# Recurrent chain of a bidirectional RWKV-7 mixer: matrix products regrouped by the form of the array they use, heads alternating, one PSUM bank for each direction's y

## The chip, the cores and the metric

One core of one Trainium2 chip runs the whole kernel. The metric is the device time of one execution in microseconds, as the median of several runs.

## The reference, cut to what matters

The reference runs two layers of a backbone over 256 context and 256 latent tokens (width 1024). Each layer has a SwiGLU half step, three mixers side by side (mLSTM, RWKV-7, differential attention) with a gated merge, and a second SwiGLU half step. The change touches only the RWKV-7 mixer. For each of 8 heads of width 64 and for each of two directions it runs this recurrence over the tokens, first over the context, then over the latent tokens:

```python
def step(s, inp):
    rt, wt, kt, vt, kkt, at = inp
    sa = jnp.einsum('bhvk,bhk->bhv', s, -kkt)
    s = s * wt[:, :, None, :] + sa[..., None] * (kkt * at)[:, :, None, :] + vt[..., None] * kt[:, :, None, :]
    return s, jnp.einsum('bhvk,bhk->bhv', s, rt)
```

The outputs of the two directions are added. The backward direction goes through the context from its end to its start and then through the latent tokens the same way.

## The kernel before, in words

The 512 tokens are cut into 8 chunks of 64 (chunks 0 to 3 context, 4 to 7 latent). The 8 heads are worked on as 4 tiles of two heads: head 0 on partitions 0 to 63, head 1 on 64 to 127. For each tile t four parts follow one another: `rwkv_cols` (dense projections), `rwkv_stage1` (elementwise work and a few products), `rwkv_stage2` (the score products "A", masks and transposes), `rwkv_solve` (a triangular inverse, mostly on VectorE), and `rwkv_chain`, the recurrence over chunks. `rwkv_post` ends the tile.

`rwkv_stage2` makes for each direction d, each half g of the chunks and each head h one PSUM bank pA: four products with a contraction over the 64 partitions of the head and 128 columns (shown by the profile as 64\*128). Three VectorE instructions then mask it into Z, Ma and Mr. The bank comes from the tag "c", which has two buffers.

`rwkv_chain` takes 8 steps; step i works on chunk i of the forward direction and on the matching chunk of the backward one. A step is: X = Ma·UV + ar·S (products of 64 by 64, one for each head and direction, shown as 64\*64), a VectorE copy of X, U = Bt·X (64\*64), two copies of U into UV (VectorE for head 0's half, ScalarE for head 1's), the state products S from UV and BK (contraction over 128 partitions, 64 columns, shown as 128\*64), and two VectorE instructions that make the next S. The output y of a chunk is Mr·UV (128\*64) plus ar·S (64\*64), accumulated in PSUM; then VectorE adds it to `ry` or ScalarE copies it there. y is written as a function `out` that is kept in `pending` and called in the next step behind the products of X. In the second layer y is wanted for latent tokens only: steps 0 to 3 have none. Each fp32 product is two matmul instructions with a weight load each.

PSUM has eight banks by tag: two "d", three "m", two "c", one "s". In the chain X, U, S and Y all take "c". The "s" bank serves `rwkv_stage1` (its products kkn, lw, la).

The order of the instructions on each engine is not written by hand: a scheduler goes through the program with a priority for each instruction and a model of time, and emits for each engine a fixed order. The chain, `rwkv_stage1` and `rwkv_solve` stand under `tc.high_priority()`; the other work of the layer (attention, mLSTM, gate tiles, merge; all dense products go through L102) is emitted in portions, `run(BUDGET[l][t][0])` and `[1]`, and fills TensorE where the chain isn't ready. What is left runs in `run(1e9)` behind the last chain. `mm` at L102 issues all products but those of U (L1116) and of the solve (L1067, L1080).

Of the kernel before, what the change touches and what calls it, by code (L numbers as in the profile page):

```python
# [35 lines left out]
# columns of the packed per-partition parameters  # L36
# [3 lines left out]
# columns of the packed constants  # L40
# [10 lines left out]
# per layer: gate tiles after each attention and mLSTM head; other work (in us of TensorE) before and after  # L51
# the columns of each next recurrent tile
# [28 lines left out]
class Halves:  # L81
    """a unit's 1024 columns in two tiles"""
# [9 lines left out]
class Builder:  # L92
# [36 lines left out]
    def unit(self, spec):  # L129
        """hi and lo parts of a unit; exact together"""  # L130
# [16 lines left out]
    def unit_early(self, spec):  # L147
        """a unit in room that the feed-forward part doesn't need yet"""
        raw = self.fp.tile([P, 1024], F32, name="araw", tag="araw", bufs=4)
        self.unit_load(raw, spec)  # L150
        r = []
        for i, tag in enumerate(("uh", "ul")):
            r.append(Halves([self.fp.tile([P, 1, NT], F32R, name=tag, tag=tag, bufs=14) for _ in range(2)]))
        for n in range(2):
            c = slice(n * NT, (n + 1) * NT)
            self.split(r[0][:, c], r[1][:, c], raw[:, c])
        return r
# [4 lines left out]
    def fm_tile(self, spec, lo=0, h=None, ps=None):  # L162
        """one feature-major tile of 128 columns: PSUM [128 cols, tokens]"""
# [17 lines left out]
    def fm_first(self, units, pss, parts):  # L181
        """the first tiles after a norm: every feature block goes to all of them as soon as it is there"""
# [10 lines left out]
    def split(self, hi, lo, src):  # L193
        """exact split of src: hi carries the leading half of the significand"""
        self.nc.scalar.copy(hi, src)
        self.nc.vector.tensor_tensor(lo, src, hi.bitcast(F32), op=ALU.subtract)  # L196

    def rsqrt(self, out, in_, eps, scale=1.0):
        """out = 1/sqrt(scale*in + eps)"""
# [8 lines left out]
    def ada_first(self, i, j):  # L208
        """block j of modulation vector i (0 shift, 1 scale) of the first norm, on TensorE"""
# [18 lines left out]
    def ada_first_shift(self, j):  # L228
        """the shift on VectorE"""
# [13 lines left out]
    def load_c(self, after=lambda: None):  # L243
        """silu of the two condition vectors on every partition"""
# [23 lines left out]
    def ada_steps(self):  # L268
        """the others on VectorE: one block of 128 outputs at a time"""
# [27 lines left out]
    def sqrt_ahead(self):  # L297
        """has ScalarE's table for the square roots of the next norm loaded before they are due"""
# [4 lines left out]
    def sumsq(self, k, c):  # L303
        """adds the squares of x_k to the running sum of these tokens"""
# [9 lines left out]
    def norm_stats(self, parts):  # L314
        """1 / rms of these tokens on every partition, in PSUM"""
# [16 lines left out]
    def norm_apply(self, l, i, k, psr, parts):  # L332
        """feature block k of the modulated norm, split into hi and lo"""
# [12 lines left out]
    def norm_mod(self, l, i, parts):  # L346
        """norm and modulation of these tokens"""
# [5 lines left out]
    def x_update(self, l, gi, k, ps, c):  # L353
        """x_k += 0.5 * gate * ps"""
# [12 lines left out]
    def ffn(self, l, which, lo, ready, after):  # L367
        """ready: the PSUM tiles of the first gate and up tiles;
        after: token ranges with what to do when x has its final value there"""
# [60 lines left out]
    def conv(self, out, ps, w, lo=0):  # L430
        """out = centred 3-tap convolution of ps; w: three [128,1] taps"""
# [35 lines left out]
    def tm_group(self, cols, consume, t0=0):  # L467
        """token-major product with 256 columns (cols: (c0, width) ranges): PSUM [128 tokens, 256]
        for each of the token tiles from t0 on"""
# [19 lines left out]
    def attn_qk(self, h):  # L489
        """raw q and k of a head, token-major (token tile, q or k), and the sums of their squares"""  # L490
# [14 lines left out]
    def attn_qk_pair(self, hp):  # L505
        """the same for two heads without the context's q: slots k0 k1 q2 k2 q3 k3 of the token tiles"""
# [32 lines left out]
    def attn_rot(self, qkr, ss):  # L539
        """normalised and rotated q and k of a head, feature-major"""  # L540
# [104 lines left out]
    def mlstm_steps(self):  # L645
# [21 lines left out]
        # gates: rows 0-3 i fwd, 32-35 i bwd, 64-67 f fwd, 96-99 f bwd (others zero)  # L667
# [27 lines left out]
        # m = F + G; em = exp(-m); nG = -G, its hi part on the first half of the partitions, lo on the other  # L695
# [20 lines left out]
        for h in range(4):  # L716
# [16 lines left out]
            # s-block j: scores against the query tokens it can reach  # L733
# [9 lines left out]
            for j in range(4):  # L743
# [3 lines left out]
                for d in range(2):  # L747
                    # reachable query blocks
# [66 lines left out]
    def rwkv_small(self):  # L815
# [6 lines left out]
        # hi and lo parts of a direction on the two halves of the partitions  # L822
# [59 lines left out]
    def rwkv_stage1(self, t, r, k, v, lw, g2):  # L882
        """everything that is elementwise over (channel, token)"""
# [5 lines left out]
        # normalised keys  # L889
# [5 lines left out]
        # 1 / max(norm, 1e-12)  # L895
# [50 lines left out]
    def rwkv_stage2(self, t, r, k, v, g2, kk, eC, dirs):  # L946
# [6 lines left out]
        # token-major v and the u of each chunk: head 0 has v on partitions 0-63 and u on 64-127,  # L953
        # head 1 the other way round. Token window w is tokens 64w-64 .. 64w+64
# [6 lines left out]
        for d in range(2):  # L961
# [6 lines left out]
            for g in range(2):  # L968
                for h in range(2):
                    pA = self.psc("A")  # L970
                    hr = slice(64 * h, 64 * h + 64)
                    for n in range(4):
                        c = 4 * g + n
                        self.mm(pA[:, n * P : (n + 1) * P], bk[hr, c].rearrange("p a b -> p (a b)"),
                                ar[hr, d, c].rearrange("p a b -> p (a b)"), True, True)
                    pv4 = pA.rearrange("p (n x) -> p n x", n=4)
# [24 lines left out]
        # bonus  # L1001
# [7 lines left out]
    def rwkv_solve(self, t, Zf):  # L1009
        """Bt[(h, s), (d, c), t] = transpose of (I - A)^-1, A strictly triangular in (t, s)"""  # L1010
        nc, a = self.nc, self.a2
        Bt = self.Bts[t % 2]
        # Zf[(h, s), (d, c), t]: the diagonal blocks first
# [7 lines left out]
        # backward units: transpose within the block so that every unit is strictly lower in (row, col)  # L1021
# [6 lines left out]
        # two sets of columns in turn, so that VectorE always has an independent instruction  # L1028
# [13 lines left out]
        # back: R[row, u, col]  # L1042
# [6 lines left out]
        # forward units: Rn = T (t, s), Rt = T^T; backward units: Rn = T^T, Rt = T  # L1049
# [5 lines left out]
        # off-diagonal blocks  # L1055
# [33 lines left out]
    def rwkv_chain(self, t, g2, Mr, Ma, BK, UV, ar, eC, bon):  # L1089
# [7 lines left out]
        S = pending = None  # L1097
        for i in range(8):
            cs = [order[0][i], order[1][i]]
            px = self.psc("X")  # L1100
            for d in range(2):
                c = cs[d]
                for h in range(2):
                    hr = slice(64 * h, 64 * h + 64)
                    self.mm(px[hr, d * 64 : d * 64 + 64], Ma[hr, d, c], UV[hr, c, h], True, i == 0)
                    if i:
                        self.mm(px[hr, d * 64 : d * 64 + 64], ar[hr, d, c, 0], S[hr, d], False, True)
            if pending:
                pending()
            X = a.tile([P, 2, 64], F32, name="X", tag="X", bufs=2)  # L1110
# [8 lines left out]
            both = (lambda x: x[:, cs[0] :: st][:, 0:2]) if st > 0 else (lambda x: x[:, cs[0] :: st][:, 0:2])  # L1119
# [9 lines left out]
            def out(i=i, cs=cs, S=S):  # L1129
                if cs[0] < lc and cs[1] < lc:  # L1130
                    return
                py = self.psc("Y")
                for d in range(2):
                    c = cs[d]
                    for h in range(2):
                        hr = slice(64 * h, 64 * h + 64)
                        self.mm(py[hr, d * 64 : d * 64 + 64], UV[:, c, h], Mr[:, d, c, h], True, i == 0)
                        if i:
# [429 lines left out]
```

## Time and profile before

| | |
|---|---|
| median of 3 runs | 2867.44 us (2856.05 to 2876.06) |
| span of the profiled execution | 2880.2 us |
| TensorE busy | 2784.9 us, 97% |
| VectorE busy | 1862.6 us, 65% |
| ScalarE busy | 1146.1 us, 40% |

The profiled execution has no time of its own beside its span; the span is 12.8 us above the median of the runs and 4.1 us above the slowest of them. A matmul counts as busy from its start until its result is in PSUM, so a busy TensorE isn't one at its peak. The two mixer stages lie at about 426 to 1238 us (layer 0) and 2026 to 2700 us (layer 1).

### The profile page before, as it was taken

To read this page: it belongs to the slowest core of one execution; us is meant where nothing else is said; L and a number is where in the kernel's file an instruction comes from. 1 tells how busy PE (TensorE), PEld (TensorE's weight loads), DVE (VectorE), ACT (ScalarE), POOL (GpSimd) and SP (SyncE) were. 2 spreads that over 40 slices of the span, in tenths; PEclk is the share of its full clock that TensorE was granted. 3 is DMA by queue.
4 is the path that set the end of the run, shared out by engine and by line. 5 is a ranking of instruction groups with operands and counts; after the bars stand their busy time and mean duration, and the time that the engine had idled before them with its cause. 6 is when DMAs were issued, how large, how long until landed. Compare 5 with 4: busy or idle time off the path is not lost.

```text
span 2880.2 us, 43519 instructions
## 1 busy us (share of the span) xinstructions
PE 2784.9 (97%) x17198; PEld 2280.8 (79%) x17198; DVE 1862.6 (65%) x3611; ACT 1146.1 (40%) x1955; POOL 236.5 (8%) x330
## 2 busy tenths in 40 slices
PE   7999999999999999999999999999999899998999
PEld 5888887668676677688888888888878677878999
DVE  7999368474593663589995443333877677746654
ACT  3322244443553543343222332222554546444543
POOL 0000002111110200200000000000212121112000
PEclk9999999799997999999999999999989899989999
DMA  7777322111121222666773232222221121226454
GB/s 264 237 238 227 100 94 68 34 63 39 59 75 41 70 74 80 225 205 221 237 240 109 88 102 96 95 95 74 98 78 57 61 65 57 92 92 214 162 183 147
DMA packets 102432, 349.65 MB, mean 121 GB/s; under 512 B 13362, under 2 KB 17842, under 8 KB 101972
## 3 DMA queue, kind: packets, MB, share of 16 engines
q1 hardware_dynamic: 91872, 315.10, 33.5%
q0 software_dynamic: 9024, 31.60, 3.3%
q8 instruction: 135, 2.21, 0.3%
q14 instruction: 69, 0.57, 0.1%
q10 hardware_dynamic: 1332, 0.18, 0.0%
HBM read 327.82 MB, written 19.01 MB: 120 GB/s over the span
## 4 chain that ended last, share of the span: by engine, by line
PE 60%; DVE 8%; issue 4%; ACT 3%; DMA 2%; POOL 1%; DVEq 0%; POOLq 0%; ACTq 0%; SPq 0%
PE d L102 25%; PE m L102 22%; PE Y L102 2%; PE A L102 2%; DVE lo L144 1%; PE X L102 1%; DVE op L1038 1%; DVE T L1041 1%; DMA yin<-yd 1%; DMA raw<-in_ws 1%; PE mo L102 1%; PE aS L102 1%; PE S L102 1%; PE U L1116 1%; ACT hi L140 1%
## 5 line engine op out<-in xcount | busy, mean ns | idle before, releaser
L140 ACT CAST hi<-raw 128x1024 fp32r<-128x1024 f32 x430 | 451.0, 1049 | 1022.0 <-PE m L102 468.0
L144 DVE TENSOR_TENSOR lo<-raw,hi 128x1024 fp32r<-128x1024 f32 (+1 forms) x508 | 544.6, 1076 | 322.7 <-ACT hi L140 315.6
L102 PE MATMUL m<-hh,hi 128*128 128x512 f32 (+1 forms) x1440 | 510.8, 357 | 3.9 <-ACT hh L342 2.5
L102 PE MATMUL m<-hl,hi 128*128 128x512 f32 (+1 forms) x1440 | 513.2, 357 | 0.0
L102 PE MATMUL m<-hh,lo 128*128 128x512 f32 (+1 forms) x1440 | 512.5, 357 | 0.0
L102 PE MATMUL d<-hh,hi 128*128 128x256 f32 (+1 forms) x976 | 357.5, 367 | 4.0 <-DVE x L359 2.7
L102 PE MATMUL d<-hl,hi 128*128 128x256 f32 (+1 forms) x976 | 353.1, 362 | 0.4 <-DVE hl L196 0.4
L102 PE MATMUL d<-hh,lo 128*128 128x256 f32 (+1 forms) x976 | 349.1, 358 | 0.1
L239 DVE SCALAR_TENSOR_TENSOR ajunk<-araw,scb 128x1024 f32<-128x1024 f32 x272 | 332.5, 1222 | 5.1 <-ACT scb L266 0.5
L102 PEld LDWEIGHTS m<-hh,hi 128*128 128x128 f32 x1440 | 272.0, 190 | 45.3 <-ACT hh L342 3.1
L102 PEld LDWEIGHTS m<-hh,lo 128*128 128x128 f32 x1440 | 272.8, 190 | 40.2 <-DVE lo L144 0.2
L102 PEld LDWEIGHTS m<-hl,hi 128*128 128x128 f32 x1440 | 272.8, 190 | 39.9 <-issue 0.2
L102 PE MATMUL d<-ul,hi 128*128 128x512 f32 (+1 forms) x770 | 269.3, 350 | 0.0
L102 PE MATMUL d<-uh,hi 128*128 128x512 f32 (+1 forms) x770 | 268.5, 349 | 0.0
L102 PE MATMUL d<-uh,lo 128*128 128x512 f32 (+1 forms) x770 | 268.3, 349 | 0.0
L102 PEld LDWEIGHTS d<-hh,hi 128*128 128x128 f32 x976 | 191.9, 197 | 37.5 <-issue 8.2
L102 PEld LDWEIGHTS d<-hl,hi 128*128 128x128 f32 x976 | 191.7, 196 | 34.5 <-issue 12.7
L102 PEld LDWEIGHTS d<-hh,lo 128*128 128x128 f32 x976 | 191.9, 197 | 26.3 <-issue 5.1
L102 PEld LDWEIGHTS d<-uh,hi 128*128 128x128 f32 x770 | 145.1, 188 | 20.8
L102 PEld LDWEIGHTS d<-ul,hi 128*128 128x128 f32 x770 | 145.4, 189 | 19.7
L102 PEld LDWEIGHTS d<-uh,lo 128*128 128x128 f32 x770 | 144.9, 188 | 19.9
L102 PE MATMUL d<-lo,hh 128*128 128x256 f32 x480 | 142.9, 298 | 0.0
(357 smaller groups left out, 4268.3 us busy)
## 6 DMA issues: line engine op xcount, KB each, us to landing
raw<-in_ws SPq DMA_DIRECT2D x430, 512.0 KB, 3.4
araw<-in_ws SPq DMA_DIRECT2D x146, 512.0 KB, 4.4
gd<-gth POOLq DMA_DIRECT2D x24, 256.0 KB, 2.5
gth<-gd SPq DMA_DIRECT2D x24, 256.0 KB, 2.9
xd<-x POOLq DMA_DIRECT2D x2, 2048.0 KB, 7.9
gd<-gth POOLq DMA_DIRECT2D x24, 128.0 KB, 2.0
gth<-gd SPq DMA_DIRECT2D x24, 128.0 KB, 3.3
yin<-yd POOLq DMA_DIRECT2D x11, 256.0 KB, 4.6
```

What stands on the lines that cost most here:

```text
L102: self.nc.tensor.matmul(out, lhsT=lhsT, rhs=rhs, start=start, stop=stop)
L140: self.nc.scalar.copy(hi, raw)
L144: self.nc.vector.tensor_tensor(lo[:, c], raw[:, c], hi[:, c].bitcast(F32), op=ALU.subtract)
L239: self.nc.vector.scalar_tensor_tensor(junk, raw, 1.0, self.scb[:, st], op0=ALU.mult, op1=ALU.mult, accum_out=self.mods[l][:, s, k, st : st ...
L1038: nc.vector.tensor_tensor(w, A[:, i + 1 :, i : i + 1].broadcast_to(w.shape), T[:, i : i + 1, c].broadcast_to(w.shape), op=ALU.mult)
L1041: nc.vector.tensor_tensor(t, t, w, op=ALU.add)
L1116: self.nc.tensor.matmul(pu[ur, d * 64 : d * 64 + 64], lhsT=Bt[hr, 8 * d + cs[d]], rhs=X[hr, d], start=True, stop=True, tile_position=(hr.s ...
```

## The change

Three places change; comments and docstrings are dropped too, so line numbers move.

- `rwkv_stage2`: for each direction and half, the banks of both heads are taken at once, and the heads alternate from product to product. The three VectorE instructions of each bank follow as before.
- X: for each direction first ar·S of both heads, then Ma·UV of both heads (before: for each head Ma·UV, then ar·S).
- y: Mr·UV of both directions is issued right behind the state products of the same step. ar·S follows in the next step behind the products of X, with the copies (function `y_state`). Each direction's y has its own bank: one from "c", one from "s".

```diff
@@ rwkv_stage2
             for g in range(2):
+                pAs = [self.psc("A") for _ in range(2)]
+                for n in range(4):
+                    c = 4 * g + n
+                    for h in range(2):
+                        hr = slice(64 * h, 64 * h + 64)
+                        self.mm(pAs[h][:, n * P : (n + 1) * P], bk[hr, c].rearrange("p a b -> p (a b)"),
+                                ar[hr, d, c].rearrange("p a b -> p (a b)"), True, True)
                 for h in range(2):
-                    pA = self.psc("A")
                     hr = slice(64 * h, 64 * h + 64)
-                    for n in range(4):
-                        c = 4 * g + n
-                        self.mm(pA[:, n * P : (n + 1) * P], bk[hr, c].rearrange("p a b -> p (a b)"),
-                                ar[hr, d, c].rearrange("p a b -> p (a b)"), True, True)
-                    pv4 = pA.rearrange("p (n x) -> p n x", n=4)
+                    pv4 = pAs[h].rearrange("p (n x) -> p n x", n=4)
@@ rwkv_chain
+        def y_state(py, cs, S):
+            if S is not None:
+                for d in range(2):
+                    for h in range(2):
+                        hr = slice(64 * h, 64 * h + 64)
+                        self.mm(py[d][hr, :64], S[hr, d], ar[hr, d, cs[d], 1], False, True)
+            for d in range(2):
+                c = cs[d]
+                if c in seen:
+                    nc.vector.tensor_tensor(y[:, c], y[:, c], py[d][:, :64], op=ALU.add)
+                else:
+                    nc.scalar.copy(y[:, c], py[d][:, :64])
+                    seen.add(c)
...
             px = self.psc("X")
             for d in range(2):
                 c = cs[d]
+                if i:
+                    for h in range(2):
+                        hr = slice(64 * h, 64 * h + 64)
+                        self.mm(px[hr, d * 64 : d * 64 + 64], ar[hr, d, c, 0], S[hr, d], True, False)
                 for h in range(2):
                     hr = slice(64 * h, 64 * h + 64)
-                    self.mm(px[hr, d * 64 : d * 64 + 64], Ma[hr, d, c], UV[hr, c, h], True, i == 0)
-                    if i:
-                        self.mm(px[hr, d * 64 : d * 64 + 64], ar[hr, d, c, 0], S[hr, d], False, True)
+                    self.mm(px[hr, d * 64 : d * 64 + 64], Ma[hr, d, c], UV[hr, c, h], i == 0, True)
             if pending:
                 pending()
+                pending = None
...
-            def out(i=i, cs=cs, S=S):
-                if cs[0] < lc and cs[1] < lc:
-                    return
-                py = self.psc("Y")
+            if not (cs[0] < lc and cs[1] < lc):
+                py = [self.psc("Y"), self.pss("Y")]
                 for d in range(2):
-                    c = cs[d]
                     for h in range(2):
                         hr = slice(64 * h, 64 * h + 64)
-                        self.mm(py[hr, d * 64 : d * 64 + 64], UV[:, c, h], Mr[:, d, c, h], True, i == 0)
-                        if i:
-                            self.mm(py[hr, d * 64 : d * 64 + 64], S[hr, d], ar[hr, d, c, 1], False, True)
-                for d in range(2):
-                    c = cs[d]
-                    if c in seen:
-                        nc.vector.tensor_tensor(y[:, c], y[:, c], py[:, d * 64 : d * 64 + 64], op=ALU.add)
-                    else:
-                        nc.scalar.copy(y[:, c], py[:, d * 64 : d * 64 + 64])
-                        seen.add(c)
-            pending = out
+                        self.mm(py[d][hr, :64], UV[:, cs[d], h], Mr[:, d, cs[d], h], True, i == 0)
+                if i:
+                    pending = lambda py=py, cs=cs, S=S: y_state(py, cs, S)
+                else:
+                    y_state(py, cs, None)
```

## Rows read from the trace of the kernel before

**Rows 1.** The page's first part: busy time, share of the span, instructions.

```profile
PE 2784.9 (97%) x17198; PEld 2280.8 (79%) x17198; DVE 1862.6 (65%) x3611; ACT 1146.1 (40%) x1955; POOL 236.5 (8%) x330
```

**Rows 2.** Windows: length, busy PE, PEld, DVE, ACT, POOL, granted clock, DMA, GB/s.

```profile
426.00:1238.00 812.00, 777.53 (x4987) 582.33 (x4986) 492.32 (x1078) 354.52 (x685) 118.79 (x146) 0.93 0.24 78
1113.00:1238.00 125.00, 118.78 (x511) 91.98 (x510) 68.34 (x110) 47.35 (x80) 25.21 (x33) 0.99 0.59 190
676.00:730.00 54.00, 54.00 (x477) 39.63 (x477) 21.41 (x59) 13.43 (x36) 4.53 (x4) 1.00 0.13 45
790.00:890.00 100.00, 91.53 (x561) 68.10 (x559) 75.43 (x160) 51.82 (x90) 11.33 (x17) 0.91 0.20 67
1070.00:1113.00 43.00, 43.00 (x400) 29.01 (x399) 12.90 (x38) 7.56 (x21) 2.54 (x5) 1.00 0.18 59
2026.00:2700.00 674.00, 636.86 (x4963) 531.48 (x4963) 471.91 (x1119) 337.23 (x637) 111.73 (x163) 0.92 0.29 93
```

**Rows 3.** Timeline of one chain step, layer 1: start, us, engine, line, out<-in.

```profile
2580.46 0.26 ACT L1122 COPY UV<-U 64x128 f32<-64x128 f32 x1 [0.81 <-DVE UV L1121]
...
2581.37 0.45 PE L102 MATMUL S<-UV,BK 128*64 128x64 f32 x6
2581.75 0.33 PE L102 MATMUL X<-UV,Ma 64*64 64x64 f32 x2
...
2582.00 0.39 PE L102 MATMUL d<-hh,lo 128*128 128x256 f32 x1
2582.18 0.29 DVE L1158 TENSOR_TENSOR S<-S,eC 128x128 f32<-128x128 f32 x1
...
2582.55 0.33 PE L102 MATMUL Y<-Mr,UV 128*64 128x64 f32 x2
2582.81 0.33 PE L102 MATMUL Y<-ar,S 64*64 64x64 f32 x2
2583.07 0.33 PE L102 MATMUL Y<-Mr,UV 128*64 128x64 f32 x2
...
2583.33 0.27 PE L102 MATMUL X<-S,ar 64*64 64x64 f32 x1
...
2584.15 0.29 DVE L1111 COPY X<-X 128x128 f32<-128x128 f32 x1 [1.68 <-PE X L102]
...
2585.30 0.28 PE L102 MATMUL d<-hh,hi 128*128 128x256 f32 x1
2585.51 0.45 PE L1116 MATMUL U<-X,Bt 64*64 64x64 f32 x8
2585.89 0.39 PE L102 MATMUL d<-hl,hi 128*128 128x256 f32 x1
...
2586.11 0.28 PE L102 MATMUL d<-hh,lo 128*128 128x256 f32 x1
2586.23 0.28 PE L102 MATMUL m<-yh,hi 128*128 128x256 f32 x1
```

**Rows 4.** Windows of tile Y alone, both mixer stages: PE, PEld, DVE, ACT.

```profile
426.00:1238.00 812.00, 64.45 (x480) 44.89 (x480) 5.63 (x32) 5.32 (x32) 0.93 0.24 78
2026.00:2700.00 674.00, 34.39 (x256) 24.25 (x256) 2.82 (x16) 2.62 (x16) 0.92 0.29 93
```

**Rows 5.** Windows of tile A alone, sum of both mixer stages (PE first).

```profile
sum 1486.00, PE 72.80 PEld 62.12 DVE 161.79; mean PE 36.40 PEld 31.06 DVE 80.89
```

**Rows 6.** Instructions on tile A: count, ns min/median/max, first and last start.

```profile
L979 DVE TENSOR_TENSOR Z<-A,cst x64: 417/423/427, 449.9 to 2497.0; 64x256 f32<-64x256 f32 x64
...
L983 DVE TENSOR_TENSOR Mr<-A,cst x64: 403/416/426, 450.7 to 2497.9; 128x256 f32<-128x256 f32 x64
```

**Rows 7.** Timeline of TensorE at 1021 us, two blocks of A.

```profile
1021.60 1.71 PE L102 MATMUL A<-ar,bk 64*128 64x128 f32 x16
1023.24 0.38 PE L102 MATMUL d<-hi,hh 128*128 128x256 f32 x1
...
1024.12 1.13 PE L102 MATMUL A<-ar,bk 64*128 64x128 f32 x8
```

More of the change, by code (lines that the diff above doesn't have):

```diff
@@ L1118, in rwkv_chain @@
             st = cs[1] - cs[0]
-            both = (lambda x: x[:, cs[0] :: st][:, 0:2]) if st > 0 else (lambda x: x[:, cs[0] :: st][:, 0:2])
+            both = lambda x: x[:, cs[0] :: st][:, 0:2]
             pu2 = pu[:, :128].rearrange("p (d x) -> p d x", d=2)
@@ L1159, in rwkv_chain @@
                 S = Sn
-        pending()
+        if pending:
+            pending()
         return t, y, g2, bon
```

## Prediction

> **What bounds the kernel now.** I read the page's busy times first: TensorE 97% of the span, VectorE 65%, ScalarE 40% [rows 1]. Busy says little by itself, so the next view is the table of windows [rows 2]. In windows that hold only the chain, TensorE has no idle time at all (54.00 of 54 us, 43.00 of 43), while VectorE works in 40% and 30% of them. In a window of score products and solve (790 to 890 us) TensorE idles 8.5 us of 100 and VectorE works 75. Over both mixer stages the idle time is 34 and 37 us of 812 and 674. Behind layer 0's last chain there are still 125 us of dense work, 119 of them busy. So the mixer stages are bound by TensorE's queue, nearly everywhere.
>
> The timeline of one step shows what that queue spends its time on, and that the recurrence waits for it rather than the reverse [rows 3]. UV is complete at 2580.72 (2580.46 + 0.26), and the last six state products start at 2581.37: 0.65 us in the queue. The state is updated at 2582.47, the first product of X with it starts at 2583.33: 0.86 us. The copy of X ends at 2584.44, U starts at 2585.51: 1.07 us. That is 2.58 us a step by which TensorE is late. What I take out of the queue shortens the step until these three are used up.
>
> In the same rows y is the costly part. Its products go two by two, Mr·UV (128\*64), ar·S (64\*64), Mr·UV, and each pair of instructions starts 0.26 us after the pair before. The eight instructions of U, which have one form and alternate heads, take 0.45 us together, of which one lasts 0.27 by itself (as the first X product): 0.18 / 7 = 0.026 us for each further one. A change of form costs TensorE far more than the products do.
>
> **The change, part by part.** First the price of a block that stands alone between dense products [rows 3]. Dense products start 0.12 us apart (2586.11 to 2586.23). Into U it is 0.21 (0.09 more), U to the next dense one 0.38, and the dense one after that 0.22 (0.10 more): 0.57 us. Eight instructions that join a block of their own form cost 8 x 0.026 = 0.21.
>
> *y.* Steps with both parts: 7 for each of 4 tiles in layer 0, 4 for each of 4 in layer 1 = 44; the counts agree, 480 and 256 instructions (the first step of layer 0 has eight) [rows 4]. Before, a step costs 4 x 0.52 (2582.55 to 2583.07) + 0.09 + 0.10 = 2.27 us. 44 of them are 100 us, and the windows show 64.45 + 34.39 = 98.84. After, Mr·UV is ready at the moment the state products are (both need UV alone) and has their form: 0.21. ar·S uses the old state, so nothing holds it until the next X; a scheduler that takes what is ready puts it right behind Mr·UV, a block alone: 0.57. Together 0.78, which saves 1.49 x 44 = 66 us. Ends: both alone, 1.14, 50 us; both joined (ar·S with X), 0.42, 81 us. I take 66.
>
> *X.* Today two instructions of Ma·UV go ahead, while the state is being updated: 0.25 us from 2581.75 to 2582.00. With ar·S first they can't, and join X's block: 2 x 0.026. That is 0.20 x 56 steps (7 in each of 8 chains) = 11 us. Ends 0 and 11. I take 11. Nothing is late for it: X needed the state before, too.
>
> *A.* The 64 blocks of eight are busy for 72.80 us, 1.14 each [rows 5]. Where the last products of one head met the first of the next, sixteen took 1.71 instead of 1.13 + 8 x 0.123 (0.123 being (1.13 - 0.27) / 7) = 2.11 [rows 7]: two heads run at the same time on the two halves of the rows. With full alternation sixteen should take what eight take now, 32 blocks instead of 64, 37 us less. But VectorE needs three instructions for each bank, two kinds of which take 0.42 us [rows 6]; 3 x 0.42 = 1.26 is more than TensorE's 1.13, and with both banks of "c" taken at once TensorE can't fill one while the other is drained. So the stage isn't shorter, and only dense work that happens to be ready turns the freed time to use; in the window of such a stage 8.5% was idle already. Ends 0 and 37; I take half, 18, since dense work was ready for most but VectorE has little room.
>
> A rule of the Trainium skill speaks against this part. TensorEngine Tiling (Array Packing), section PSUM Bottleneck, says that packing speeds up the products and not the emptying of PSUM, which may then bound. The rows agree so far (1.26 against 1.13); by the rule A would give 0, and the sum would be 18 less.
>
> *Banks.* U now takes the bank of "c" that y's first direction leaves, so U waits for its copy. Behind U on TensorE everything waits. If y's copy is late each time by one such copy (0.26, as the UV copy), that is 44 x 0.26 = 11 us; if ar·S runs early, 0. I take 5. The second direction holds "s" from behind S until at most the next U (2581.37 to 2585.51, 4.1 us), which `rwkv_stage1` uses for five products. That collides where stage 1 of the next tile runs beside a chain with y. At worst 5 x 4.1 = 21 us in a tile, but as a delay of the recurrence, and the 125 us of dense work behind layer 0's last chain cover it: 0. Without that cover the 21 us would count. The copies of y are as many as before. No DMA, SyncE or GpSimd instruction moves.
>
> *Sum.* 66 + 11 + 18 - 5 = 90 us, 3.1% of the profiled span. 2880.2 - 90 = 2790; the median of the runs lies 12.8 below that span, so 2867.4 - 90 = **2777 us**. Per step with y about 1.7 us leave the queue, less than the 2.58 by which it is late, so the recurrence doesn't become the bound.
>
> **The rivals.** *VectorE keeps A's gain.* The mechanism is above: 1.26 us of masks for a bank against 1.13 of products. For it: VectorE works 75 of 100 us there. Against: the idle time of TensorE is only 8.5. It gives 66 + 11 - 5 = 72, so 2795.
>
> *The blocks don't stay together.* The scheduler orders by its own model; it already splits the state products (six of the eight stand in one row, two went ahead). If it splits Mr·UV and ar·S likewise with dense work between, a piece of two costs 0.25 + 0.09 + 0.10 = 0.44, one of six 0.57 - 0.05 = 0.52, so y costs 1.92 a step and saves 0.35 x 44 = 15; the X gain is lost the same way. 15 + 18 - 5 = 28, so 2839. Against: the state products split because the second head's UV comes later, and Mr·UV has both.
>
> *The clock, slower than before.* The granted clock is 0.93 and 0.92 over the mixer stages: (1 - 0.93) x 2 x 812 + (1 - 0.92) x 2 x 674 = 222 us at 1.2 GHz instead of 2.4 [rows 2]. The chain windows in the rows have 1.00, the solve's window 0.91. If chains with tighter small products count as quiet like the solve, some 340 us more of the chains (8 of about 50 us, part of them low already) go to 1.2 GHz; each such microsecond loses half: +170 - 90 = +80, 2947. It decides from 180 us more at 1.2 GHz, that is a granted clock of 0.865 in place of 0.925. Against: the change removes stalls between products and adds none.
>
> **How the numbers follow.** Forecast 0.58 (own range 2755 to 2805: y between its ends, A between 10 and 30), A's gain kept by VectorE 0.20, blocks apart 0.14, clock 0.08. A measurement of this kernel tells about 1% from no change: faster is below 2839. The first two and half of the third are faster: 0.85; the other half the same: 0.07; slower 0.08. With the upper ends of y, X and A (81 + 11 + 37) the time would be 2738; the range is 2750 to 2838, which leaves out the clock, half of the blocks apart and the joined ends.
>
> **What would show it.** After the change: Mr·UV right behind the state products in one run of 128\*64; y's busy sum at about 98.84 x 0.78 / 2.27 = 34 us; blocks of sixteen A in about 1.15 us; no early pair of Ma·UV; chain steps with y shorter by about 1.7 us; TensorE still without idle time in chains. I would be wrong if the blocks are scattered, if U waits visibly for a copy of y, if TensorE's idle time in score stages grows by what A frees, or if the granted clock falls.

## The result and the profile after

The change takes 2797.45 us in the median of 4 runs (2791.73 to 2807.59) against 2871.22 for the kernel before, measured beside it (4 runs, 2856.05 to 2876.06): a ratio of 0.9742, 95% interval 0.9700 to 0.9784. The forecast was 2777, range 2750 to 2838. So direction and range held; 90 us were forecast and 74 came. What the 74 are made of is another matter than the prediction said. Its rival "VectorE keeps A's gain" had named almost this time, 2795, but TensorE spent hardly less on A, so there was no gain for VectorE to keep (see the experiments on A).

The first part of the page after answers to [rows 1]:

```profile
PE 2689.3 (96%) x17198; PEld 2220.3 (79%) x17198; DVE 1855.8 (66%) x3611; ACT 1145.2 (41%) x1954; POOL 237.5 (8%) x330
```

TensorE is busy 95.6 us less (2784.9 to 2689.3), but the span is only 74.4 shorter (2880.2 to 2805.8): its idle time grew by 21.2, from 95.3 to 116.5. The windows of the two mixer stages, which answer to the first and last of [rows 2], show where:

```profile
425.00:1190.00 765.00, 723.20 (x5001) 547.54 (x5000) 494.69 (x1081) 356.54 (x688) 118.59 (x146) 0.95 0.25 83
1976.00:2660.00 684.00, 632.25 (x5244) 541.78 (x5244) 485.07 (x1141) 352.50 (x659) 112.97 (x163) 0.94 0.31 101
```

Idle 41.8 and 51.8 us, where it was 34 and 37; and the granted clock is 0.95 and 0.94 in place of 0.93 and 0.92. Tile Y in the same windows (compare [rows 4]) is busy for 29.72 + 17.19 = 46.91 us; it was 98.84, and 34 was forecast:

```profile
425.00:1190.00 765.00, 29.72 (x480) 23.99 (x480) 5.94 (x32) 5.60 (x32) 0.95 0.25 83
1976.00:2660.00 684.00, 17.19 (x256) 13.56 (x256) 3.07 (x16) 2.62 (x16) 0.94 0.31 101
```

One chain step of layer 1 on TensorE (timeline, compare [rows 3]):

```profile
2541.07 0.45 PE L1138 MATMUL U<-X,Bt 64*64 64x64 f32 x8
...
2542.24 0.33 PE L102 MATMUL S<-UV,BK 128*64 128x64 f32 x2
2542.41 0.28 PE L102 MATMUL Y<-Mr,UV 128*64 128x64 f32 x2
2542.62 0.39 PE L102 MATMUL d<-hh,lo 128*128 128x256 f32 x1
2542.93 0.39 PE L102 MATMUL S<-UV,BK 128*64 128x64 f32 x5
2543.10 0.22 PE L102 MATMUL Y<-Mr,UV 128*64 128x64 f32 x1
2543.15 0.22 PE L102 MATMUL S<-UV,BK 128*64 128x64 f32 x1
2543.16 0.45 PE L102 MATMUL Y<-Mr,UV 128*64 128x64 f32 x5
2543.54 0.45 PE L102 MATMUL Y<-ar,S 64*64 64x64 f32 x8
2543.92 0.39 PE L102 MATMUL d<-hh,hi 128*128 128x256 f32 x1
...
2545.07 0.33 PE L102 MATMUL X<-S,ar 64*64 64x64 f32 x4
...
2545.46 0.28 PE L102 MATMUL X<-UV,Ma 64*64 64x64 f32 x4
2545.68 0.39 PE L102 MATMUL d<-hh,lo 128*128 128x256 f32 x1
...
2546.34 0.45 PE L1138 MATMUL U<-X,Bt 64*64 64x64 f32 x8
```

As forecast: Mr·UV joins S, from 2542.93 to 2543.54 twelve instructions of one form in a row (four went ahead; by the program they are head 0's, whose half of UV is copied first); ar·S follows at once as a block of eight, long before X; X is sixteen instructions in 0.61 us (2545.07 to 2545.68) with no early pair of Ma·UV; nothing waits for a copy of y.

**Two measures for what follows.** Runs of one and the same kernel differ, and by their clock: in 22 runs of the kernel before, the time goes from 2857.34 us at a granted clock of 0.971 to 2885.81 at 0.961. A run's time multiplied by its clock is an estimate of what it would take at 2.4 GHz throughout, if all that runs at 1.2 GHz took half as long there. I call it the time at full clock. For one kernel it hardly moves: over those 22 runs it is 2774.0 with a standard deviation of 2.7, and in two later sets of 11 and 10 runs 2774.0 and 2774.9. So each time splits into work and clock: before 2774.0 and 98 lost to the clock (2871.8 - 2774.0, mean of the 22); after 2725.1 and 73.5 (mean 2798.6). The gain of 73 between these means is 49 of work and 24 of clock.

The second measure splits TensorE's time by tile: from each instruction's start to the next one's, without the idle part, each stretch multiplied by the clock granted in it, summed over the profiled execution (us; one execution of each kernel):

| | Y | S | X | A | idle |
|---|---|---|---|---|---|
| before | 85.5 | 30.5 | 51.3 | 64.9 | 87.8 |
| after | 39.3 | 22.3 | 36.7 | 63.2 | 107.1 |
| y alone | 41.7 | 22.4 | 47.3 | 64.5 | 108.8 |
| X alone | 86.5 | 32.2 | 37.2 | 65.4 | 94.1 |
| A alone | 84.2 | 31.4 | 52.4 | 63.3 | 92.4 |
| y and X | 39.3 | 22.3 | 36.5 | 65.0 | 101.3 |
| A forced to alternate | 40.1 | 21.4 | 36.2 | 46.6 | 117.0 |
| one bank for y | 37.4 | 25.8 | 37.5 | 64.9 | 90.1 |
| heads in turn | 41.9 | 22.7 | 52.9 | 62.6 | 104.6 |

### The profile page after: what moved, and what is told of

Its sections match the earlier page's. It is cut to its first block, busy times and chain, and to the rows that moved or that the text cites. A ratio compares the mean times of both kernels' runs of the same rounds, so it can differ in the third digit from the quotient of the medians.

```text
span 2805.8 us, 43561 instructions
## 1 busy us (share of the span) xinstructions
PE 2689.3 (96%) x17198; PEld 2220.3 (79%) x17198; DVE 1855.8 (66%) x3611; ACT 1145.2 (41%) x1954; POOL 237.5 (8%) x330
## 4 chain that ended last, share of the span: by engine, by line
PE 79%; DVE 10%; ACT 4%; issue 3%; DMA 2%; POOL 2%; ACTq 0%; DVEq 0%; POOLq 0%; SPq 0%
PE d L102 33%; PE m L102 32%; PE A L102 2%; PE X L102 1%; DVE lo L144 1%; PE Y L102 1%; PE mo L102 1%; DVE op L1041 1%; DVE T L1044 1%; PE S L102 1%; PE aS L102 1%; PE U L1138 1%; DMA yin<-yd 1%; DVE bk L942 1%; PE ay L102 1%
## 5 line engine op out<-in xcount | busy, mean ns | idle before, releaser
L102 PE MATMUL d<-hh,hi 128*128 128x256 f32 (+1 forms) x976 | 349.7, 358 | 3.7 <-ACT tw L824 0.8
L102 PE MATMUL d<-hl,hi 128*128 128x256 f32 (+1 forms) x976 | 344.0, 353 | 0.2 <-DVE hl L196 0.2
L102 PEld LDWEIGHTS d<-hh,hi 128*128 128x128 f32 x976 | 186.9, 191 | 36.5 <-issue 9.8
L102 PEld LDWEIGHTS d<-hl,hi 128*128 128x128 f32 x976 | 186.9, 191 | 31.4 <-issue 11.0
L102 PEld LDWEIGHTS d<-hh,lo 128*128 128x128 f32 x976 | 186.8, 191 | 31.4 <-issue 7.2
L102 PE MATMUL d<-hi,hh 128*128 128x256 f32 x480 | 147.3, 307 | 3.2 <-DVE mz L439 3.2
```

Of the source, the lines that this page charges most:

```text
L102: self.nc.tensor.matmul(out, lhsT=lhsT, rhs=rhs, start=start, stop=stop)
```

## The experiments

All of them are measured beside the kernel before. The kernels' times (clock and time at full clock are means over the runs):

| | median us (runs) | ratio to before, 95% | clock | at full clock |
|---|---|---|---|---|
| y alone | 2838.88 (6) | 0.9903 (0.9877 to 0.9929) | 0.966 | 2743.5 |
| X alone | 2855.73 (11) | 0.9934 (0.9903 to 0.9965) | 0.971 | 2766.5 |
| A alone | 2857.90 (12) | 0.9952 (0.9930 to 0.9974) | 0.973 | 2779.9 |
| y and X | 2817.30 (5) | 0.9826 (0.9795 to 0.9856) | 0.966 | 2719.8 |
| A forced to alternate | 2824.91 (5) | 0.9807 (0.9777 to 0.9837) | 0.960 | 2712.2 |
| one bank for y | 2773.02 (6) | 0.9621 (0.9589 to 0.9654) | 0.978 | 2711.7 |
| y and X, heads of A swapped | 2805.34 (6) | 0.9750 (0.9715 to 0.9784) | 0.970 | 2723.5 |
| all, heads of A swapped | 2798.33 (6) | 0.9713 (0.9683 to 0.9742) | 0.971 | 2717.7 |
| one bank, without A | 2801.65 (6) | 0.9751 (0.9701 to 0.9800) | 0.969 | 2716.8 |
| one bank, A forced | 2797.80 (6) | 0.9738 (0.9696 to 0.9781) | 0.968 | 2707.2 |
| heads in turn | 2809.98 (4) | 0.9782 (0.9718 to 0.9846) | 0.977 | 2743.9 |
| one bank, ar·S behind X | 2774.62 (6) | 0.9665 (0.9619 to 0.9711) | 0.977 | 2712.3 |

### The parts by themselves

**y alone.** X and A as in the kernel before.

```diff
-                if i:
-                    for h in range(2):
-                        self.mm(px[hr, ...], ar[hr, d, c, 0], S[hr, d], True, False)
                 for h in range(2):
-                    self.mm(px[hr, ...], Ma[hr, d, c], UV[hr, c, h], i == 0, True)
+                    self.mm(px[hr, ...], Ma[hr, d, c], UV[hr, c, h], True, i == 0)
+                    if i:
+                        self.mm(px[hr, ...], ar[hr, d, c, 0], S[hr, d], False, True)
...
-                pAs = [self.psc("A") for _ in range(2)]
+                    pA = self.psc("A")
```

> Only the y part of the change: Mr·UV behind S, ar·S as a block, a bank for each direction; X and A as before. Theory (runs of one form): in the order that TensorE is given, the short products of the chain stand in 626 runs of one form before (351 of 64*64, 275 of 128*64), 283 after, and here in 328 (223 and 105), so 298 of the 343 runs that the change removes are gone. The tiles X, S, U and Y took 212 us from start to start before and 134 after, 78 for 343 runs, 0.23 each. So 298 x 0.23 = 68 us less TensorE time in the chains here, and with the part that turned into idle time after, a time of about 2871 - 50 = 2815 to 2825. By the prediction's own term (66) 2805. Rival (the clock carries it): the granted clock rose from 0.93/0.92 to 0.95/0.94 in the mixers after; if that came from X or A, it is 0.93/0.92 here and the gain is under 40, above 2830.

It missed: 2838.88, not 2815 to 2825. Y and S fell by 43.8 and 8.1 and X by 4.0, 56 of the 68 us expected of TensorE; 21 us came back as idle time, and 30.5 at full clock are left. The clock stayed at 0.966. The rival's time came true, and its reason in part: some of the whole change's gain is clock, and it isn't y that brings it. The other part of the miss is the idle time, which the rival did not name.

**X alone.** The kernel before with the order of X from the change.

```diff
                 for h in range(2):
-                    self.mm(px[hr, ...], Ma[hr, d, c], UV[hr, c, h], True, i == 0)
-                    if i:
-                        self.mm(px[hr, ...], ar[hr, d, c, 0], S[hr, d], False, True)
+                    self.mm(px[hr, ...], Ma[hr, d, c], UV[hr, c, h], i == 0, True)
```

> Only the X part: ar·S of both heads, then Ma·UV of both heads; y and A as before. Theory: the short products stand in 578 runs of one form instead of 626, 48 x 0.23 = 11 us, and the X products alternate heads in pairs: 2855 to 2863. The prediction's term gives the same 11, 2860. Rival: without the early Ma·UV the step gets longer where X was already waited for; then no gain, 2871.

2855.73, as expected. X itself fell by 14.1, at full clock the kernel by 7.5, since 6 us came back as idle time. The rest of the time's gain is clock, which in these 11 runs goes from 0.964 to 0.981, further than in the runs of any other kernel.

**A alone.** The kernel before with `rwkv_stage2` from the change:

```diff
+                pAs = [self.psc("A") for _ in range(2)]
+                for n in range(4):
+                    for h in range(2):
+                        self.mm(pAs[h][:, ...], bk[hr, c]..., ar[hr, d, c]..., True, True)
```

> Only the score products A regrouped; chain as before. Theory: the scheduler undoes the alternation, because the two banks of c come free one after the other: in the order given to TensorE, A stands in 53 blocks before and 53 here, of one head each. Then the time is that of before, 2871 within 6 us, and A stays busy for 72 to 77 us in all. The prediction's term would give 18 less, 2853. Rival (taking both banks at once holds the stage up): slower by up to 10.

Neither theory: 2857.90, a gain of 0.5% with an interval clear of 1. But A hardly got cheaper (64.9 to 63.3), and at full clock the kernel is 5.9 slower. What it gained is clock: 0.970 to 0.975 in its 12 runs, 0.961 to 0.971 in the 22 of before.

**y and X.** The change without that diff.

> The change without its A part. Theory: A's part is worth nothing (its blocks stand in the same order), so this kernel takes the time of the whole change, 2797 within 6 us. By the prediction's term of 18 for A: 2815. If holding both banks costs something: under 2792.

2817.30, so the term of 18 seemed to hold after all. At full clock, though, this kernel is at 2719.8, no worse than the whole change (2725.1); all that it lacks is clock, 0.966 against 0.974.

### A: work or clock?

**A forced to alternate.** Edges hold the sixteen products of two banks in the order head 0, head 1, head 0, ...

```diff
                     for h in range(2):
-                        self.mm(pAs[h][:, ...], bk[hr, c]..., ar[hr, d, c]..., True, True)
+                        ins = self.mm(pAs[h][:, ...], bk[hr, c]..., ar[hr, d, c]..., True, True).ins
+                        if last is not None:
+                            self.tc.add_manual_dep(ins, last.name, NoSync, reason="alternate")
+                        last = ins
```

> The whole change, with edges that force the order of the score products: head 0, head 1, head 0, ... in each pair of banks, so that the heads really alternate. In these numbers time at full clock is a run's time multiplied by its granted clock (before 2774, the change 2725). Theory (A is a cost of TensorE): sixteen instructions take what eight took, A falls from 63 us at full clock to about 35 and the time at full clock to about 2700, 2775 us at a clock of 0.974. Rival (VectorE keeps the gain, 1.26 us of masks for a bank against 1.13 of products; both banks must be free first): A falls as well, but idle time grows by as much, and the time at full clock stays at 2725 or rises to 2740.

Without the edges nearly all of A stands as before, in blocks of eight or two such blocks in a row (54 blocks with A alone, 53 before). The reason that I give for it is an argument from the program and not from a run: the two banks of c come free one after the other, and the scheduler issues what is ready, all products of the first bank, then all of the second. With the edges the timeline shows fourteen instructions in the time that eight took [rows 7]:

```profile
446.50 0.46 PE L102 MATMUL A<-ar,bk 64*128 64x128 f32 x2 [0.21 <-DVE bk L942]
...
448.19 1.13 PE L102 MATMUL A<-ar,bk 64*128 64x128 f32 x14 [0.68 <-DVE bk L942]
449.24 0.50 PE L102 MATMUL la<-tas,lorah 128*128 128x512 f32 x1
```

Tile A's sum over both mixer stages (compare [rows 5]: 72.80) in the whole change, and then with the edges:

```profile
sum 1449.00, PE 77.11 PEld 65.83 DVE 161.26; mean PE 38.55 PEld 32.91 DVE 80.63
```

```profile
sum 1489.00, PE 55.81 PEld 43.60 DVE 158.87; mean PE 27.91 PEld 21.80 DVE 79.44
```

So in the profiled executions the real alternation saves 17 us of A at full clock and gives 10 back as idle time; over the runs the time at full clock falls by 13 (2725.1 to 2712.2). But the clock falls from 0.974 to 0.960, and the kernel is 27 us slower. The rule that the prediction names from the Trainium skill (TensorEngine Tiling (Array Packing), section PSUM Bottleneck) says that after packing the emptying of PSUM may bound. For A's own banks the trace doesn't show it: the idle time in front of A rose by 1 us only (9.7 to 10.6 at full clock). More lies in the chains (1.7 to 7.2), where U, S and X now wait 9 us in all for VectorE's copies and updates, and not at all without the edges; that the masks hold these up is not shown (us in all, times, longest):

```profile
PE U L1145 <- DVE X L1140: 3.4, 8, 0.5
PE S L102 <- DVE UV L1150: 3.1, 8, 0.4
...
PE X L102 <- DVE S L1178: 2.4, 3, 0.8
```

**Heads of A swapped.** Two neutral edits: head 1's bank first, in the kernel without the A part (diff) and likewise, for products and masks, in the whole change.

```diff
-                for h in range(2):
+                for h in (1, 0):
                     pA = self.psc("A")
```

> The change without its A part, and the two heads' banks of A simply filled in the other order (head 1 first). Nothing else is changed, and no price differs. Theory (the A part raises the clock by its form): granted clock 0.966 and 2817 us, as without this swap. Rival (the clock hangs on how the stages happen to fall, and any edit of the order moves it): the clock is off from 0.966 by 0.003 or more, with the time at full clock still at 2720.

> The whole change, with head 1 ahead of head 0 in the score products and their masks. Theory (the A part raises the clock by its form): granted clock 0.974 and 2797 us. Rival (the clock hangs on how the stages happen to fall): the clock is off from 0.974 by 0.003 or more, down to 0.966, where the time is 2820; time at full clock 2725 either way.

The swap moved the clock by 0.004 (0.966 to 0.970) and by 0.003 (0.974 to 0.971), and the time at full clock by 4 and 7 us. So an edit of the order that changes no price is worth some 10 us either way; single differences of that size say nothing.

**Over all kernels** there is a pattern, though. The six kernels without the A part (before, y, X, y and X, its swap, one bank without A) have mean clocks of 0.963 to 0.971 (before itself 0.966, 0.963 and 0.966 in its three sets); the six with it, unforced, 0.971 to 0.978; the two with forced alternation 0.960 and 0.968. Four pairs differ by the A part alone: it goes with 0.007 more clock by itself, 0.008 in the change and 0.009 with one bank, but with the heads swapped only with 0.001 to 0.002 (0.970 and 0.971). The four times are 15, 20, 29 and 7 us shorter with it. One place where the stretches at 1.2 GHz go away lies behind the first solve. Windows before that solve's last products and from there into the chain, first in the kernel before, then with A alone, y and X, and the whole change:

```profile
496.00:510.00 14.00, 11.18 (x47) 8.33 (x46) 12.04 (x44) 3.92 (x11) 0.59 (x1) 0.88 0.43 132
510.00:545.00 35.00, 34.93 (x241) 21.47 (x241) 11.57 (x26) 15.57 (x34) 2.06 (x5) 0.56 0.07 23
```

```profile
496.00:510.00 14.00, 11.33 (x46) 8.05 (x45) 11.64 (x45) 4.32 (x12) 0.59 (x1) 0.88 0.41 132
510.00:545.00 35.00, 35.00 (x358) 23.27 (x356) 17.78 (x38) 22.74 (x49) 4.06 (x8) 1.00 0.08 24
```

```profile
496.00:510.00 14.00, 11.39 (x50) 8.32 (x46) 12.75 (x45) 3.92 (x11) 0.59 (x1) 0.88 0.45 132
510.00:545.00 35.00, 35.00 (x362) 23.50 (x362) 13.80 (x34) 16.72 (x39) 2.06 (x5) 0.80 0.08 24
```

```profile
496.00:510.00 14.00, 11.32 (x52) 7.89 (x50) 13.16 (x47) 4.66 (x13) 0.59 (x1) 1.00 0.41 133
510.00:545.00 35.00, 35.00 (x444) 24.23 (x442) 18.37 (x45) 21.00 (x46) 2.61 (x6) 1.00 0.10 32
```

TensorE did nearly the same in the 14 us ahead (11.2 to 11.4 us busy in all four), and then was granted 0.56, 1.00, 0.80 and 1.00. In the 35 us that follow it is hardly ever idle in any of them, but gets 241, 358, 362 and 444 instructions done: a busy share of 100% says nothing of the clock. Why the A part shifts these stretches stays open, since its blocks are nearly as many (54 and 53, or 58 both in the change and in y and X) and as dear as without it: the traces show that the clock is higher with it, not what it is in it.

### y's second bank

**One bank for y.** Both directions share a bank of c again, and s is left to stage 1. Direction 1's products go without start, behind those of direction 0, so that both are one accumulation group.

```diff
-                py = [self.psc("Y"), self.pss("Y")]
+                pyc = self.psc("Y")
+                py = [pyc[:, 0:64], pyc[:, 64:128]]
...
-                        self.mm(py[d][hr, :64], UV[:, cs[d], h], Mr[:, d, cs[d], h], True, i == 0)
+                        m = self.mm(py[d][hr, :64], UV[:, cs[d], h], Mr[:, d, cs[d], h], d == 0, i == 0 and d == 1)
+                        if d:
+                            self.behind(m, m0[h])      # an edge: order only
...
-                        self.mm(py[d][hr, :64], S[hr, d], ar[hr, d, cs[d], 1], False, True)
+                        m = self.mm(py[d][hr, :64], S[hr, d], ar[hr, d, cs[d], 1], False, d == 1)
```

> The whole change, with y of both directions in one bank of c, as before, and the bank s left to stage 1. Theory (the bank s): in the order that TensorE is given, stage 1 of the next tile (kkn, lw, la) lies inside the running chain for 4 of 6 tiles before and for none after the change, since y holds s; there its waits come on top of those of the group norm behind the chain (gv 4.0 us of idle time before, 14.5 after; la 2.1 and 6.3). Here it is inside again for 4 tiles, so gv and la fall to about 5 and 2 and the idle time from 116 to about 100: time at full clock 2710, 2782 us at a clock of 0.974. Rival (idle time grew because shorter chains use up less of the cover): gv and la stay, 2797. Other rival (one bank less for y makes U wait for both copies): slower than 2800.

2773.02, the lowest median of all, and at full clock the 2710 that were expected (2711.7). The list of TensorE's waits shows the two that were meant, gv and la, and a third behind the chain, m (us in all, times, longest), first before, then after, then here:

```profile
PE m L102 <- ACT yh L195: 6.2, 4, 2.4
...
PE gv L102 <- ACT gsq L1174: 4.0, 2, 2.4
...
PE la L102 <- ACT w L914: 2.1, 1, 2.1
```

```profile
PE gv L102 <- ACT gsq L1188: 14.5, 5, 4.0
PE m L102 <- ACT yh L195: 13.1, 6, 4.4
...
PE la L102 <- ACT w L914: 6.3, 4, 2.1
```

```profile
PE gv L102 <- ACT gsq L1202: 7.6, 3, 3.5
PE m L102 <- ACT yh L200: 6.7, 4, 3.2
PE X L102 <- DVE S L1185: 6.6, 6, 1.6
...
PE la L102 <- ACT w L919: 2.1, 1, 2.1
```

After the change, kkn (stage 1's first product) of the next tile starts only behind the chain's last U in four tiles where it lay inside the chain before, and stage 1's waits (la) fall together with those of the group norm (gv), where little else is ready. With s free, stage 1 lies inside the chain again in these four tiles and hides; in exchange X waits 6.6 us for S. That VectorE has stage 1's work in between is the likely reason and not shown. The idle time at full clock is back at 90 (before 88, after 107). At full clock the kernel gains 13 (2725.1 to 2711.7).

**One bank, without A.** The diff above, with `rwkv_stage2` as before the change.

> y of both directions in one bank (as in the run with one bank for y: 2773 us, granted clock 0.978, time at full clock 2712), and the A part left out. The A part cost about 5 us at full clock so far (2780 against 2774 alone, 2725 against 2720 in the whole), and the clock stood 0.002 to 0.008 higher with it than without. Theory (A's form gives clock): full clock 2707, clock 0.971 to 0.974, 2785 us. Rival (the clock goes by how the stages fall, A only shuffles it): full clock 2707 with a clock that may as well be 0.978 or more, 2768.

The clock fell as the theory had it, and a little further (0.969, not 0.971 to 0.974); its work did not come: 2716.8 at full clock where 2707 was expected. Against y and X with two banks (2719.8) the one bank is worth only 3 here, against 13 in the pair above. So its waits are shown to go, but its worth at full clock is no better known than 3 to 13. All traces agree on the waits: gv, la and m take 12 to 22 us together in the seven kernels that leave s to stage 1, and 31 to 41 in the seven that hold y in s. In the pair without A they fall by 25 us, but other waits take their place, and the idle time falls by 4 only.

**One bank, A forced.** The diff above, and the edges of the forced alternation.

> One bank for y, and the heads of A forced to alternate. On the whole change, forcing took 13 us at full clock (2725 to 2712: A itself 63 to 47, idle time up by 10) but the granted clock fell from 0.974 to 0.960, so it was 27 us slower. Theory (the denser A leaves idle time behind it, and the clock falls after it): full clock 2699, clock lower than 0.978 by about 0.01, 2785 us. Rival (that fall of the clock was how the stages happened to fall): full clock 2699 at 0.975 or more, 2765 or less.

Both forced kernels are short on clock (0.960 and 0.968, against 0.974 and 0.978 unforced), so it is hardly chance; at full clock forcing was worth 5 here (2711.7 to 2707.2), no more than the heads' swap moved (4 and 7).

### What the grouping is worth, and what the alternation

**Heads in turn.** The same runs of one form as in the change, but inside them all of head 0, then all of head 1.

```diff
-                for d in range(2):
-                    for h in range(2):
+                for h in range(2):
+                    for d in range(2):
                         hr = slice(64 * h, 64 * h + 64)
                         self.mm(py[d][hr, :64], UV[:, cs[d], h], Mr[:, d, cs[d], h], True, i == 0)
```

and likewise for y's ar·S and for X.

> The whole change with the same runs of one form (184 of 64*64, 102 of 128*64), but the heads don't alternate inside them: all products of head 0, then all of head 1, in y and X. Theory (form and alternation each have a price; in one form two instructions of the same head start 58 ns apart, two of different heads 29 on the mean): Y rises from 39 us at full clock to about 57, X from 37 to about 51, as X was before the change; time at full clock 2725 + 32 = 2757. Rival (only the form counts, as the prediction's price of 0.026 for any further instruction has it): 2725, Y 39, X 37.

X shows it best (timeline of one step): sixteen instructions from 2545.03 to 2545.93, 0.90 us in place of 0.61. By their starts only the first four and the last four come one by one (58 ns apart from the second on); the eight between them overlap and take 0.29 us, so the scheduler did not keep the order all through.

```profile
2545.03 0.33 PE L102 MATMUL X<-S,ar 64*64 64x64 f32 x2
2545.20 0.28 PE L102 MATMUL X<-UV,Ma 64*64 64x64 f32 x2
2545.32 0.33 PE L102 MATMUL X<-S,ar 64*64 64x64 f32 x4
2545.43 0.33 PE L102 MATMUL X<-UV,Ma 64*64 64x64 f32 x4
2545.60 0.28 PE L102 MATMUL X<-S,ar 64*64 64x64 f32 x2
2545.72 0.28 PE L102 MATMUL X<-UV,Ma 64*64 64x64 f32 x2
2545.93 0.39 PE L102 MATMUL m<-yh,lo 128*128 128x256 f32 x1
```

X is at 52.9 us, as before the change (51.3), though nothing of Ma·UV goes ahead any more. Y rose by 2.6 only, not 18: ar·S still alternates in the trace (starts 13 and 45 ns apart in turn), and part of Mr·UV falls between products of S, so for y this test is weak. At full clock the grouping by form, with the alternation that is left, gives 30 (2774 to 2743.9), and the alternation that this edit takes away another 19.

**One bank, ar·S behind X.** Edges from X's last product to each ar·S of y.

```diff
-                pending()
+                pending(mx)          # mx: the last product of X; in y_state
...
+                        if mx is not None:
+                            self.behind(m, mx)
```

> One bank for y, and edges that hold y's ar·S back until it is behind the last product of X, whose form it has (146 runs of 64*64 instead of 185). Theory (a block alone costs 0.57, a joined one 0.21): 44 x 0.36 = 16 us less, time at full clock 2712 - 16 = 2696. Rival (U takes the bank that y leaves, and now waits for both copies of y each time, 44 x 0.3 = 13 us): 2709, with idle time in front of U, or slower than 2712.

The rival held: 2712.3 at full clock. Y and X fell by 1.8 and 3.8, and the idle time rose by 9, nearly half of it in front of U (4.3 us in place of 0.4):

```profile
PE U L1149 <- DVE X L1144: 4.3, 3, 3.3
```

## Why the prediction was right, and where it wasn't

The time fell into the range by luck, because two errors partly cancel: the work gave 49 us where 90 were forecast, and the clock gave 24 where none was. At full clock the terms come out, in the profiled executions, as 54 for y with S, 15 for X, 2 for A and -19 for idle time, 51 together.

**y, 66.** Right in its mechanism, too large in its size. y itself saved 46.2 us at full clock, under the lower end of 50; with the 8.2 that S saved it is 54, 12 short of the value taken. The term that was mis-sized is the price of before, 2.27 us a step: y took 85.5 / 44 = 1.94. The busy sum of 98.84 seemed to confirm the 2.27, but busy counts a product beyond the next one's start (0.33 us for pairs 0.26 apart) and at the clock of 0.92 to 0.93. y after, forecast at 0.78, is 39.3 / 44 = 0.89, since S and Mr·UV come in two pieces: "Mr·UV has both" holds no longer once it stands right behind S. S's own 8 us came unpriced.

**X, 11.** The size is right (14.6), the reason isn't. The step that failed is the early pair of Ma·UV as the whole gain: without that pair but with the heads mostly in turn, X costs 52.9 as before. What pays is that ar·S of head 0 and head 1 follow each other, and Ma·UV likewise.

**A, 18.** The step that failed is "with full alternation sixteen should take what eight take now": the diff asks for it, TensorE's order hasn't got it. A fell by 1.7. Forced, it holds in the blocks shown, fourteen in 1.13 us, and A falls by 17; the time at full clock is 13 and 5 lower, 0 to 37 having been the ends, but the clock takes that back. What went with the A part instead is clock, 0.007 to 0.009 in three pairs, some 20 us, and nearly none in the fourth. That this comes near the 18 is an accident.

**Banks, 5, and the collision, 0.** U waits for no copy of y (0.1 us). The collision on s was seen and then set to nothing: "the 125 us of dense work behind layer 0's last chain cover it: 0". That step failed: the stage was pushed back in four tiles, three of them in layer 1, which that cover doesn't reach. gv, m and la wait 22 us longer, and TensorE's idle time grew by 21. That this is the figure of the worst case is chance: the worst case meant 21 us in one tile, by a delay of the recurrence. One bank brought back 17 of the idle time in one pair and 4 in the other, so how much of the 21 the collision cost stays open.

**The clock.** The rival was there with the other sign only: slower at 0.865. It went to 0.95 and 0.94. That tighter chains would lower it, nothing shows: y alone left the clock where it was.

**What would show it.** Held: Mr·UV behind S, no early Ma·UV, no idle time in the chains, steps with y in layer 1 shorter. From U to U they take 8.5 us before and 4.9 after, on the mean of 12 in the profiled executions. Of these 3.6 the chain's own products are 1.6, where 1.7 were forecast; the other 2.0 are work of other tiles that no longer falls into the step and is done elsewhere. Not held: Y at 34 us, blocks of sixteen A in 1.15. More idle time of TensorE in the score stages was among the signs of being wrong. At full clock it grew by 15 us in the 30 us behind the chains, and by 5 in the 60 us ahead of them, where A and the solve lie.

## What to carry to other kernels

Split a time into work and clock (time multiplied by the granted clock) before explaining a difference of one per cent; here that turned a term that the time seemed to confirm into a refuted one. A PSUM bank that is lent to one stage is taken from another: look at who uses that tag, and in which stage it then waits. An order asked for in the program is only had if its buffers are free together; look at the order of instructions before costing it.

## What the runs showed of the hardware

- Two products of 64\*64 on different heads start 7 and 52 ns apart in turn (29 on the mean), of the same head 58; a change between 64\*64 and 128\*64 takes 0.15 us. The Trainium skill says, in TensorEngine Tiling (Array Packing), section Key Properties, that changing the tiling mode drains TensorE; these runs put the price at about 0.1 us more than a product of the same form. In the kernel before the second product of a pair of y is late too: 0.107 us behind the first.
- The clock differs from run to run of one kernel (0.961 to 0.971), and these runs differ by 1% in time, while the standard deviation of their product is 0.1%. Two kernels with nearly the same products in another order differ by up to 0.018 in their mean clock (0.960 to 0.978).
